# A call order for SyncE, other steps in the up-projection, and which late tap comes first

## The chip, the cores and the metric

The kernel runs on one core of one Trainium2 chip, in one launch. The metric is the device time of one execution in microseconds (us). The engines are named as in the profile: PE is TensorE, DVE is VectorE, ACT is ScalarE, POOL is GpSimd, SP is SyncE, which only issues DMAs.

## The reference

Two layers (`l` = 0, 1) of an encoder over 1024 tokens of width 1024, in float32, and a last norm. Cut to what matters here:

```
for l in range(2):
    h = rmsnorm(x);  p = h @ w_in
    q, k, v from the normed latents of p (384 and 256 wide), 8 heads of 64 + 32 rotary
    y_attn = softmax(q k^T) v
    u = a * sigmoid(g)                     # 512 channels
    u = depthwise_conv(u, 31 taps)
    u = silu(layernorm(u))
    x = x + concat(y_attn, u) @ w_o
    z = depthwise_conv(rmsnorm(x) @ w_up, 3 taps)     # 1024 x 5632
    zg, zv = split(z)
    x = x + (silu(zg) * zv) @ w_down       # 2816 x 1024
return rmsnorm(x)
```

## The kernel before

Activations lie with channels on the 128 partitions and the 1024 tokens along the free dimension. To keep float32's accuracy, an operand is split into an upper part ("hi", rounded to the type TensorE multiplies) and a lower part ("lo", the rest), and a product is three matmuls: hi·hi, hi·lo, lo·hi. Each layer runs through projection, attention, output projection (wo), up-projection and down-projection. In layer 0 these begin at about 0, 200, 421, 507 and 920 us, layer 1's attention at about 1320 and its up-projection at 1628 us.

**Who orders the work.** The kernel writes out its order by hand: closures are put on numbered steps with a rank inside the step, and emitted step by step. Inside `tc.manual_schedule(engines=MANUAL)` the engines in `MANUAL` issue their instructions in the order of emission. SP is not among them, so the framework's scheduler orders SP's DMAs by its own estimates of when each can start.

**The up-projection** (`up_steps`). There are 22 blocks `f` of 128 gate features (e = 0) and 128 value features (e = 1). The tokens are in two halves, the 1024 inputs of a weight block too, and a Strassen-like scheme makes the four half-products out of seven (the sets i = 1 to 7) per block. A product (i, f) is 12 matmuls in f16 of 128 x 512 (L1221) and takes one step. The steps are numbered on from the 16 of the wo stage, so the 154 products are steps 16 to 169. The sequence is `START` for the first four blocks (`LEFT`), then for each block the sets in `ORDER`. `at[i, f]` is the step of a product, m = at[1, f] that of a block's first one.

Per block, with distances from m that stand in `UP`:

- `fetch` (SP, L1106): two raw weight blocks of 512 KB, into a buffer "wr" (e = 0) and a buffer "b" (e = 1)
- `squares` (ACT, L1128), one for each e in two steps: squares of the raw weights, for the scale of each feature; `total` (PE, L1161) sums them over the partitions, a step later DVE makes the scale (L1133 and following)
- `first_hi`, `first_lo`: sets 1 and 2, upper on ACT (L1182), lower on DVE (L1185)
- `sum5`, `sum6`, `sum3`, `sum7` (POOL, L1112): DMAs that add another quarter of the weights onto the raw buffer, in place; sum5 comes one step after the first square, sum6 after lo of 5, sum3 after lo of 6, sum7 one step after `first_lo`, onto the e = 0 buffer
- `part_hi`, `part_lo` of the sets 5, 6, 3, 7, 4 (L1182, L1185), the pair of numbers in `UP`. lo of set 7 is the last to read the e = 0 buffer, lo of set 4 the last to read the e = 1 buffer.

One step after a product `evict` takes it out of PSUM: as a copy on ACT (L1228) or as an addition on DVE (L1229). When the three parts of zg are there, the filter of 3 taps starts on ACT (L1618) and is done on DVE (L1624), one tap in each of the next two steps; `silu` (L1260, ACT) and `close` (the product of zg and zv, L1102 by `sub`) follow, and `close` also issues the store of the result to HBM (L1268). For the first four blocks the steps of the filters stand in `TAPS_AT`, gate and value. `sum_load`, `sum_step` (DVE, L1102) prepare sums of the down weights, and the last sum's step also issues their store (L1281).

**The head of attention.** Per head, q's part `pn` is multiplied on TensorE (L234), scaled out of PSUM on DVE (`qn`, L748), split by ACT (`qns`, L750) and DVE (L752); `pv` (L1653) makes v; then the scores `s` (L1677). Beside it, on an agenda `n` spread over attention, the taps of the 31-tap convolution that are left are done as "late" taps (`tap_late`), each with a buffer of its own that must have come free, of three kinds:

- "act": ACT multiplies in two halves (L1906), POOL issues a DMA that adds (L1914)
- "pool": POOL multiplies (L1909) and issues the DMA that adds
- "both": POOL multiplies and adds (L1909, L1912)

`LATE_KINDS` gives the repeating five kinds for the first and for the second half of the taps (50 in layer 0, 48 in layer 1).

Of the kernel before, what the change touches and what calls it, by code (L numbers as in the profile page):

```python
# [31 lines left out]
NF = DFF // 128  # L32
# [44 lines left out]
ROW_AT = {2: (7,)}  # L77
ROW_LATE = {0: (6,)}
E = mybir.EngineType
MANUAL = [E.PE, E.DVE, E.Activation, E.Pool]  # L80
LATE_KINDS = (("pool", "both", "act", "pool", "act"), ("pool", "both", "pool", "pool", "pool"))
LATE_COST = {"act": 1.1, "pool": 3.5, "both": 4.8}
NEAR_TAPS = (12, 14, 16, 14)
NEAR_ORDER = (0, 1, 2, 3)
# [2 lines left out]
NPAR = P_BF + 2 * NF  # L87
HALVES = (slice(0, 512), slice(512, T))
ORDER = (1, 5, 6, 3, 7, 2, 4)
LEFT = 4  # L90
START = [(i, f) for f in range(LEFT) for i in (1, 2)]
START += [(i, f) for i in (5, 3, 6, 7, 4) for f in range(LEFT)]
MIX_AT = {5: (((19, 1), (20, 0.5)), ((20, 0.4), (21, 0.5))), 3: (((23, 0.6), (24, 0.6)), ((24, 0.5), (25, 0.6))),
          6: (((26, 0.6), (27, 0.6)), ((27, 0.5), (28, 0.6))), 7: (((30, 0.6), (31, 0.6)), ((31, 0.5), (32, 0.6))),
# [3 lines left out]
KEPT = 18  # L98
TAIL_STEPS = 6
FIRST_TOTAL = 7  # L100
TOTAL_AT = 32
TAPS_AT = (36, 39, 42, 46), (44, 48, 52, 57)
UP = {'fetch': -18, 'squares': -15, 'total': -13, 1: (-2, -2), 5: (-10, -9), 6: (-5, -4), 3: (0, 1), 7: (2, 3), 4: (-1, 0)}
SUM_AT = (0, 1, 2, 6)
LEFT_AT = {5: (15, 16, 18, 19), 6: (19, 21, 22, 23), 3: (24, 25, 26, 27), 7: (25, 31, 33, 34), 4: (37, 38, 39, 40)}
ENDS = (slice(512, 768), slice(768, T))
LEAD_HEADS = 3
# [26 lines left out]
class Encoder:  # L134
# [257 lines left out]
    def run(self):  # L392
# [11 lines left out]
        carry = None  # L404
        with self.tc.manual_schedule(engines=set(MANUAL)):
            for l in range(DEPTH):
# [687 lines left out]
    def up_steps(self, l, steps, put):  # L1094
        nc, a = self.nc, self.a
        left, right = HALVES
        seq = START + [(i, f) for f in range(LEFT, NF) for i in ORDER if (i, f) not in START]
        base = len(steps)
        at = {p: base + q for q, p in enumerate(seq)}
        self.kept = {}  # L1100
        raw, wts, zs, st, sums, scale, back, nback = defaultdict(dict), {}, defaultdict(dict), {}, {}, {}, {}, {}
# [28 lines left out]
        def scales(ps, out, w):  # L1130
            ps = ps.rearrange("p (f e) -> p f e", e=2)
            scale, back, nback, v, h = (out[:, i * w:(i + 1) * w] for i in range(5))
            nc.vector.tensor_reduce(out=v, in_=ps, op=ALU.add, axis=AX.X)  # L1133
            self.half_exponent(h, v)
            self.power(scale, h, -1.0, 204.0)
            for o, at in ((back, self.back), (nback, self.nback)):
                nc.vector.tensor_scalar(out=o.bitcast(I32), in0=h.bitcast(I32), scalar1=EXPONENT, scalar2=at, op0=ALU.mult, op1=ALU.add)
            return scale, back, nback

        def first_total():  # L1140
            ps = self.bank(f"wt{l}", (128, 2 * LEFT))
            tags = self.banks[1][0]
            tags.insert(0, tags.pop())
            nc.tensor.matmul(ps, self.ones, st["sums"], start=True, stop=True)
            parts = scales(ps, self.cp.tile([128, 5 * LEFT], F32, name=f"wt{l}", tag="wt", bufs=1), LEFT)
            for f in range(LEFT):
                scale[f], back[f], nback[f] = (t[:, f:f + 1] for t in parts)
# [97 lines left out]
        def filter_start(f, e):  # L1245
            z = zs[f]
            z["ov"[e]] = o = self.blk(f"{'ov'[e]}{l}_{f}")
            z["in", e] = z.pop("gv"[e]) if e == 0 else z["src"]
            self.conv_start(l, e * NF + f, o, z["in", e], 0, T)

        def filter_tap(f, e, t):
            z = zs[f]
            self.conv_tap(l, e * NF + f, z["ov"[e]], z["in", e], 0, T, t)

        def keep(f):
            zs[f]["src"] = zs[f].pop("v")

        def silu(f):
            o = zs[f]["o"]
            nc.scalar.activation(out=o, in_=o, func=AF.Silu)  # L1260

        def close(f):
            z = zs.pop(f)
            sub(z["v"], z["v"], z["o"], ALU.mult)
            if f >= KEPT:
                self.kept[f] = z["v"]
                return
            nc.sync.dma_start(out=self.actd[l][f], in_=z["v"])  # L1268

        def sum_load(j):  # L1270
            sums[j] = [self.blk(f"sd{l}_{j}{e}") for e in range(2)]
            for e, t in enumerate(sums[j]):
                nc.sync.dma_start(out=t, in_=a["w_down"][l, j + e * (NF // 2)])

        def sum_step(j, n):
            p, q = sums[j]
            o, x = ((p[:, left], p[:, right]), (p[:, right], q[:, right]), (q[:, right], p[:, left]), (q[:, left], q[:, right]))[n]
            sub(o, o, x, ALU.add)
            if n == 3:
                for e, t in enumerate(sums.pop(j)):  # L1280
                    nc.sync.dma_start(out=self.wsd[l][j, e], in_=t)  # L1281

        def at_step(m, rank, g, *args):
            put(m, rank, lambda: g(*args))
# [11 lines left out]
        for f in range(LEFT):  # L1296
            at_step((13, 13, 15, 15)[f], 6 + f, sum5, f)
            for i, ms in LEFT_AT.items():
                m, g = ms[f], f % 2
# [4 lines left out]
        for q, (i, f) in enumerate(seq):  # L1304
            n = base + q
            steps.append(lambda i=i, f=f: product(i, f))
            m = EVICT.get((i, f), n + 1)
            put(int(m), m % 1 * 10, lambda i=i, f=f: evict(i, f))
        for f in range(LEFT, NF):
            n = m = at[1, f]  # L1310
            for e in range(2):
                at_step(m + UP["fetch"], 5 + e / 10, fetch, f, e, "b" if e else "wr")
                at_step(m + UP["squares"] + e, 2, own_squares, f, e)
            at_step(m + UP["squares"] + 1, 2.1, sum5, f)
            at_step(max(m + UP["total"], TOTAL_AT), 0.4, own_total, f)
            at_step(max(m + UP["total"], TOTAL_AT) + 1, 0.5, own_scale, f)
            for i in (5, 6, 3, 7, 4):
                hi, lo = (max(m + o, TOTAL_AT + 1) for o in UP[i])
                at_step(hi, 3.6, part_hi, i, f)
# [7 lines left out]
        for f in range(NF):  # L1327
            n = max(at[2, f], at[3, f], at[6, f]) + 1
            n = n if f >= LEFT else TAPS_AT[0][f]
            put(n, 3, lambda f=f: filter_start(f, 0))  # L1330
            put(n + 1, 3, lambda f=f: filter_tap(f, 0, 0))
            put(n + 2, 3, lambda f=f: filter_tap(f, 0, 2))
            put(n + 3, 4, lambda f=f: silu(f))
            m = max(at[7, f], at[4, f]) + 2 if f >= LEFT else TAPS_AT[1][f]
            put(m, 2.9, lambda f=f: keep(f))
            put(m, 3, lambda f=f: filter_start(f, 1))
            put(m + 1, 3, lambda f=f: filter_tap(f, 1, 0))
            put(m + 2, 3, lambda f=f: filter_tap(f, 1, 2))
            put(max(m + 3, n + 5), 3, lambda f=f: close(f))
        for j in range(NF // 2):  # L1340
            n = at[1, 7 + j * 13 // 11]
            put(n - 4, 5, lambda j=j: sum_load(j))
            for i, d in enumerate(SUM_AT):
                put(n + d, 4, lambda j=j, i=i: sum_step(j, i))

    def down_steps(self, l, steps, put):
        nc, a = self.nc, self.a
# [63 lines left out]
        def product(i, j, ms=range(4), cs=done):  # L1411
            b, t = pairs[i, j], BANK_SET[i]
            for m in ms:
                if i in (1, 5, 2) and j == 0:
                    ps[t, m] = self.pp.tile([128, 512], F32, name=f"pd{l}_{i}{m}", tag=f"d{4 * t + (m + 2) % 4}", bufs=1)
                for s, (p, q) in enumerate(((0, 0), (0, 1), (1, 0))):
                    nc.tensor.matmul(ps[t, m][:, cs], w[i, j][p][:, m * 128:(m + 1) * 128], b[:, q, cs],  # L1417
                                     start=(i in (1, 5, 2) and j == 0 and s == 0), stop=(j == half - 1 and s == 2),
                                     skip_group_check=i in (6, 7, 4, 3))
# [19 lines left out]

        order = [(i, j) for i in ORDER for j in range(half)]  # L1440
        at = {p: base + q for q, p in enumerate(order)}
# [27 lines left out]
        for c in range(2 if last else 0):  # L1469
            for m in range(4):  # L1470
                steps.append(lambda c=c, m=m: [product(4, j, (m,), cols[c]) for j in range(tail, half)])
        for i in ORDER[:-1]:
            for m in range(4):
# [166 lines left out]
    def attention(self, l, u, conv, away, spill, kvs, loaded, ahead, wo, begun):  # L1640
# [162 lines left out]
        while any(rest.values()):  # L1803
            j = max((j for j in rest if rest[j]), key=lambda j: (all(j != e for e, _ in late[-2:]), len(rest[j]), -j))
            late.append((j, rest[j].pop(0)))
        kinds = [LATE_KINDS[2 * i // len(late)][i % 5] for i in range(len(late))]
        costs, taken = [LATE_COST[kind] for kind in kinds], set()
# [247 lines left out]
```

## Time and profile before

| | us |
|---|---|
| median of 3 runs | 2264.53 |
| lowest, highest | 2263.61, 2265.57 |
| the profiled execution | 2264.85 |
| its span in the profile | 2263.0 |
| TensorE busy | 2233.7 |
| mean granted clock of TensorE | 0.999 |

The page gives each engine's busy time and the costliest groups of instructions. A group's row has: line, engine, operation, out<-in by the program's names without numbers, shapes and count; then busy us and mean ns; then the idle time of the engine just before these instructions, and who ended most of it. A row of a timeline has the start, the length, then the same, and in brackets the idle time before it and its releaser. A row of waits has who waited for whom: us in total, how often, the longest. "SPq" and "POOLq" are the queues of DMA issues.

### The profile page before, as it was taken

The page shows a single profiled execution, that of the slowest core. Times are in us where ns is not written, and L with a number is a line of the kernel's source. Part 1 is how long each engine was busy: PE and PEld are TensorE (multiplying, and loading weights), DVE is VectorE, ACT ScalarE, POOL GpSimd, SP SyncE. Part 2 cuts the span into 40 slices and gives each one's busy share as a digit, 9 for nine tenths or more (in the row PEclk, how much of TensorE's full clock was granted, in tenths as well). Part 3 has the DMA queues.
Part 4 walks back from the last instruction along what each step waited for, and adds up shares of the span by engine and source line. Part 5 has one row for each costly group of instructions (what it writes and reads, how often), then busy time and mean ns, then how long its engine had stood idle before and what let it go on. Part 6 is the DMA issues. An engine that isn't in the chain of part 4 may idle for free.

```text
span 2263.0 us, 30127 instructions
## 1 busy us (share of the span) xinstructions
PE 2233.7 (99%) x10762; PEld 1511.4 (67%) x10762; DVE 1809.0 (80%) x2484; ACT 1349.5 (60%) x2076; POOL 659.2 (29%) x632
## 2 busy tenths in 40 slices
PE   9999999999999999999999999999999999999998
PEld 8887777784444444788888877777744444448887
DVE  7989888878888887776559798887798887878665
ACT  5355987646766665544533568786467666655444
POOL 1222788511111111001412237864111111110032
PEclk9999999999999999999999999999999999999999
DMA  6887998955589796835968989878646888868356
GB/s 192 171 182 251 196 205 176 267 152 117 134 231 257 202 255 163 295 102 138 210 142 167 212 252 208 182 158 246 168 108 158 236 244 223 241 162 284 103 123 171
DMA packets 176967, 434.81 MB, mean 192 GB/s; under 512 B 24769, under 2 KB 32817, under 8 KB 176817
## 3 DMA queue, kind: packets, MB, share of 16 engines
q0 software_dynamic: 79520, 176.31, 41.7%
q1 hardware_dynamic: 97008, 256.04, 33.5%
q8 instruction: 85, 1.39, 0.3%
q14 instruction: 66, 0.53, 0.1%
q10 hardware_dynamic: 288, 0.53, 0.1%
HBM read 293.56 MB, written 80.40 MB: 165 GB/s over the span
## 4 chain that ended last, share of the span: by engine, by line
PE 71%; DVE 12%; DMA 8%; ACT 4%; issue 4%; POOL 1%; SPq 0%; DVEq 0%; POOLq 0%; ACTq 0%
PE pd L1417 18%; PE p L1221 18%; PE s L1677 7%; DMA wu<-in_w_up 5%; PE po L956 5%; PE t L1717 4%; PE o L1740 4%; PE pa L234 2%; DVE w L1185 2%; DVE v L1624 2%; PE pg L234 2%; PE pg L552 2%; DVE conv L1892 2%; PE pq L234 1%; DVE sd L1102 1%
## 5 line engine op out<-in xcount | busy, mean ns | idle before, releaser
L1221 PE MATMUL p<-b,w 128*128 128x512 f16 x3696 | 807.6, 379 | 16.6 <-DVE w L1185 12.1
L1221 PEld LDWEIGHTS <-w 128*128 128x128 f16 x3696 | 360.3, 99 | 449.0 <-DVE w L1185 22.5
L1417 PE MATMUL pd<-ab,wd 128*128 128x512 f32 (+1 forms) x1920 | 422.7, 382 | 0.0
L1417 PEld LDWEIGHTS pd<-ab,wd 128*128 128x128 f32 x1920 | 350.7, 188 | 69.7 <-DVE ab L1612 0.4
L1112 POOL DMA_DIRECT2D wu<-in_w_up x176 | 153.7, 945 | 757.2 <-DVE w L1185 370.4
L1677 PE MATMUL s<-k,q 96*128 96x512 f32 x768 | 208.2, 406 | 3.3 <-DVE qn L748 3.0
L1128 ACT ACTIVATE wsq<-wu 128x1024 f16<-128x1024 f32 x88 | 92.3, 1050 | 179.8 <-DMA wu<-in_w_up 159.3
L1720 DVE SCALAR_TENSOR_TENSOR pt<-t,pt 128x512 f16<-128x512 f32 x256 | 164.7, 684 | 39.2 <-ACT pt L1719 38.6
L1185 DVE SCALAR_TENSOR_TENSOR w<-wu,wf,w 128x512 f16<-128x512 f32 (+1 forms) x216 | 177.4, 834 | 14.6 <-ACT w L1182 14.6
L1909 POOL TENSOR_TENSOR late<-gate,par 128x1014 f32<-128x1014 f32 (+12 forms) x79 | 172.4, 2182 | 12.8 <-PE pn L234 7.1
L1719 ACT ACTIVATE pt<-t 128x512 f16<-128x512 f32 x256 | 139.2, 595 | 56.8 <-PE t L1717 55.9
L1182 ACT ACTIVATE w<-wu,wf 128x512 f16<-128x512 f32 (+1 forms) x216 | 162.5, 783 | 6.9 <-DMA wu<-in_w_up 6.8
L1679 DVE TENSOR_REDUCE mx<-s 128x1 f32<-128x1024 f32 x128 | 155.6, 1215 | 1.3 <-PE s L1677 1.3
L1624 DVE SCALAR_TENSOR_TENSOR o<-zg,par,o 128x1023 f32<-128x1023 f32 x88 | 112.6, 1280 | 53.9 <-ACT o L1618 53.7
L1677 PEld LDWEIGHTS s<-k,q 96*128 96x128 f32 x768 | 135.8, 189 | 26.4 <-DVE qn L748 3.4
L1892 DVE SCALAR_TENSOR_TENSOR conv<-gate,par,conv 128x1009 f32<-128x1009 f32 (+7 forms) x112 | 142.2, 1274 | 3.7 <-ACT conv L614 1.0
L1687 ACT ACTIVATE p<-s,mx 128x1024 f32<-128x1024 f32 x128 | 143.3, 1119 | 2.6 <-DVE mx L1679 2.2
L1610 ACT CAST ab<-ac 128x512 fp32r<-128x512 f32 x130 | 80.0, 616 | 101.6 <-DVE ac L1351 64.3
L1717 PEld LDWEIGHTS t<-ident,p 128*128 128x128 f32 x1024 | 119.7, 141 | 25.1 <-DVE yt L1747 0.8
L1740 PE MATMUL o<-pt,v 128*128 128x512 f16 x512 | 132.8, 381 | 1.3 <-DVE pt L1720 1.1
L1717 PE MATMUL t<-ident,p 128*128 128x128 f32 x1024 | 133.2, 273 | 0.1
L918 POOL DMA_DIRECT2D wd<-in_w_down x44 | 31.8, 724 | 323.6 <-PE pd L1417 322.4
(2114 smaller groups left out, 3834.9 us busy)
## 6 DMA issues: line engine op xcount, KB each, us to landing
wu<-in_w_up SPq DMA_DIRECT2D x98, 512.0 KB, 5.9
wu<-in_w_up POOLq DMA_DIRECT2D x176, 256.0 KB, 4.7
sd<-in_w_down SPq DMA_DIRECT2D x44, 512.0 KB, 6.6
ws<-sd SPq DMA_DIRECT2D x44, 512.0 KB, 4.2
wd<-in_w_down POOLq DMA_DIRECT2D x88, 256.0 KB, 5.5
act<-v SPq DMA_DIRECT2D x36, 512.0 KB, 4.5
ac<-act SPq DMA_DIRECT2D x72, 256.0 KB, 5.8
wo<-in_w_o POOLq DMA_DIRECT2D x64, 256.0 KB, 7.5
```

The source lines that it names most:

```text
L1182: nc.scalar.activation(out=t, in_=src, func=AF.Copy, scale=scale[f])
L1185: nc.vector.scalar_tensor_tensor(out=t, in0=src, scalar=scale[f], in1=hi, op0=ALU.mult, op1=ALU.subtract)
L1221: nc.tensor.matmul(ps, w[p][:, k * 128:(k + 1) * 128], b[:, q], start=(i in (1, 5, 2) and k == 0 and t == 0), stop=(k == 3 and t == 2), sk ...
L1417: nc.tensor.matmul(ps[t, m][:, cs], w[i, j][p][:, m * 128:(m + 1) * 128], b[:, q, cs], start=(i in (1, 5, 2) and j == 0 and s == 0), stop= ...
L1624: self.nc.vector.scalar_tensor_tensor(out=o[:, a:b], in0=z[:, at + a:at + b], scalar=self.par[l][:, tap:tap + 1], in1=o[:, a:b], op0=ALU.m ...
L1677: nc.tensor.matmul(ps[:, cs], q[i][0:96, qs], k[j][0:96, cs], start=(s == 0), stop=(s == 2))
L1679: nc.vector.tensor_reduce(out=mx, in_=ps, op=ALU.max, axis=AX.X, negate=True)
L1717: nc.tensor.transpose(tp[:, i, qi * 128:(qi + 1) * 128], st["p"][2 * qp + qi][:, kt * 128:(kt + 1) * 128], self.ident)
L1720: nc.vector.scalar_tensor_tensor(out=lo, in0=tp, scalar=P_SCALE, in1=hi, op0=ALU.mult, op1=ALU.subtract)
L1740: nc.tensor.matmul(po, v[2 * c + i][:, h // 2, e, :], pt[s][:, 2 * (c % 2) + i, :], start=(c == 0 and i == 0 and s == 0), stop=(c == 3 and ...
L1892: self.nc.vector.scalar_tensor_tensor(out=y[:, lo:hi], in0=u[:, lo + s:hi + s], scalar=self.tap(l, j, t), in1=y[:, lo:hi], op0=ALU.mult, o ...
L1909: self.nc.gpsimd.tensor_tensor(out=p[:, lo:hi], in0=u[:, lo + s:hi + s], in1=self.tap(l, j, t).broadcast_to([128, hi - lo]), op=ALU.mult)
```

## The change

1. SP joins `MANUAL`: its DMAs are issued in the order of emission. The two stores become closures of their own (`act_store`, `sum_store`), one step (`STORE_LAG`) after `close` and after the last `sum_step`.
2. In the first half of the late taps the kinds go act, both, pool, act, pool and not pool, both, act, pool, act; their numbers in five stay.
3. From the fifth block on the up-projection takes the sets in `UP_ORDER`: set 2 is second, 6 third, 5 fourth; 7 stays fifth, 3 goes from fourth to sixth, 4 stays last. `START` exchanges (2, 0) and (1, 1). The down-projection keeps `ORDER`.
4. In `UP`, squares, total, and the parts of 5, 6, 3 and 4 come one step later, lo of 7 and hi of 7 one step earlier; `TOTAL_AT` and `TAPS_AT` for the first four blocks change.

```diff
-MANUAL = [E.PE, E.DVE, E.Activation, E.Pool]
-LATE_KINDS = (("pool", "both", "act", "pool", "act"), ("pool", "both", "pool", "pool", "pool"))
+MANUAL = [E.PE, E.DVE, E.Activation, E.Pool, E.SP]
+LATE_KINDS = (("act", "both", "pool", "act", "pool"), ("pool", "both", "pool", "pool", "pool"))
...
 ORDER = (1, 5, 6, 3, 7, 2, 4)
+UP_ORDER = (1, 2, 6, 5, 7, 3, 4)
 LEFT = 4
-START = [(i, f) for f in range(LEFT) for i in (1, 2)]
+START = [(i, f) for i, f in ((1, 0), (1, 1), (2, 0), (2, 1), (1, 2), (2, 2), (1, 3), (2, 3))]
...
-TOTAL_AT = 32
-TAPS_AT = (36, 39, 42, 46), (44, 48, 52, 57)
-UP = {'fetch': -18, 'squares': -15, 'total': -13, 1: (-2, -2), 5: (-10, -9), 6: (-5, -4), 3: (0, 1), 7: (2, 3), 4: (-1, 0)}
+TOTAL_AT = 33
+TAPS_AT = (35, 37, 40, 46), (41, 47, 54, 60)
+UP = {'fetch': -18, 'squares': -14, 'total': -12, 1: (-2, -2), 5: (-9, -8), 6: (-4, -3), 3: (1, 2), 7: (1, 2), 4: (0, 1)}
 SUM_AT = (0, 1, 2, 6)
+STORE_LAG = 1
...
-        seq = START + [(i, f) for f in range(LEFT, NF) for i in ORDER if (i, f) not in START]
+        seq = START + [(i, f) for f in range(LEFT, NF) for i in UP_ORDER if (i, f) not in START]
...
-            nc.sync.dma_start(out=self.actd[l][f], in_=z["v"])
+            st["act", f] = z["v"]
+
+        def act_store(f):
+            if f < KEPT:
+                nc.sync.dma_start(out=self.actd[l][f], in_=st.pop(("act", f)))
...
-            if n == 3:
-                for e, t in enumerate(sums.pop(j)):
-                    nc.sync.dma_start(out=self.wsd[l][j, e], in_=t)
+
+        def sum_store(j):
+            for e, t in enumerate(sums.pop(j)):
+                nc.sync.dma_start(out=self.wsd[l][j, e], in_=t)
...
             put(max(m + 3, n + 5), 3, lambda f=f: close(f))
+            put(max(m + 3, n + 5) + STORE_LAG, 3, lambda f=f: act_store(f))
...
+            put(n + SUM_AT[-1] + STORE_LAG, 4, lambda j=j: sum_store(j))
```

## The prediction

> **What bounds the kernel now.** I read the page first, then the busy time of the two up-projections, then who makes TensorE wait, then the timelines around the largest of these waits, and last the waits of SyncE's queue.
>
> ```profile
> span 2263.0 us, 30127 instructions
> ...
> PE 2233.7 (99%) x10762; PEld 1511.4 (67%) x10762; DVE 1809.0 (80%) x2484; ACT 1349.5 (60%) x2076; POOL 659.2 (29%) x632
> ...
> L1221 PE MATMUL p<-b,w 128*128 128x512 f16 x3696 | 807.6, 379 | 16.6 <-DVE w L1185 12.1
> ...
> L1128 ACT ACTIVATE wsq<-wu 128x1024 f16<-128x1024 f32 x88 | 92.3, 1050 | 179.8 <-DMA wu<-in_w_up 159.3
> ...
> wu<-in_w_up SPq DMA_DIRECT2D x98, 512.0 KB, 5.9
> wu<-in_w_up POOLq DMA_DIRECT2D x176, 256.0 KB, 4.7
> ```
>
> TensorE is busy for 2233.7 of 2263.0 us. The change gives it no other matmuls, so all that can be won is its idle time, 29.3 us, what each stop costs beside it, and time at a low granted clock. More than half of the idle time stands before the products of the up-projection (L1221). The two stages, layer 0 and layer 1:
>
> ```profile
> 507.10:920.30 413.20, 404.69 (x1898) 185.76 (x1898) 342.30 (x478) 262.73 (x370) 70.43 (x80) 1.00 0.74 196
> 1627.70:2040.70 413.00, 404.86 (x1898) 185.80 (x1898) 342.44 (x479) 262.37 (x370) 69.31 (x80) 1.00 0.75 196
> ```
>
> The columns after the length are the busy times of PE, PEld, DVE, ACT and POOL. PE is idle for 8.51 and 8.14 us, 16.65 together; DVE is 83% busy and ACT 64%, so neither is the bound on average and the idle time is one of order. TensorE's waits name the places:
>
> ```profile
> PE p L1221 <- DVE w L1185: 12.1, 15, 1.6
> PE p L1221 <- ACT zg L1228: 3.0, 3, 1.3
> PE s L1677 <- DVE qn L748: 3.0, 1, 3.0
> PE p L1221 <- DVE b L1034: 1.3, 2, 0.6
> ```
>
> Twenty stops (15, 3 and 2) lie in the up-projections; in total 16.4 us, none longer than 1.6. One more, of 3.0 us, is at the start of layer 0's attention. A stop costs more than its idle time, since a lone matmul shows 379 ns, but in a run they follow each other faster:
>
> ```profile
> 749.67 8.15 PE L1221 MATMUL p<-b,w 128*128 128x512 f16 x37
> ...
> 764.28 0.59 PE L1221 MATMUL p<-b,w 128*128 128x512 f16 x2 [1.15 <-ACT zg L1228]
> ```
>
> (8.15 − 0.38) / 36 = 0.216 us, so each stop adds 0.38 − 0.22 = 0.16, twenty of them 3.3. Removable in both up stages: 16.65 + 3.3 = 19.9 us. A step is 12 matmuls, 12 × 0.216 = 2.59 us: longer than any stop.
>
> **Up-projection: the late weights.** The stop above is the end of this chain (ACT, then POOL, then DVE):
>
> ```profile
> 749.60 1.06 ACT L1128 ACTIVATE wsq<-wu 128x1024 f16<-128x1024 f32 x1 [5.05 <-DMA wu<-in_w_up]
> ...
> 761.38 1.33 ACT L1182 ACTIVATE w<-wu,wf 128x512 f16<-128x512 f32 x2 [2.83 <-DMA wu<-in_w_up]
> ...
> 763.57 0.67 ACT L1228 ACTIVATE zg<-p,wf 128x512 f32<-128x512 f32 x1
> ```
> ```profile
> 754.70 0.87 POOL L1112 DMA_DIRECT2D wu<-in_w_up  x1 [2.29 <-ACT wsq L1128]
> ```
> ```profile
> 762.75 0.75 DVE L1185 SCALAR_TENSOR_TENSOR w<-wu,wf,w 128x512 f16<-128x512 f32 x1 [2.80 <-ACT w L1182]
> ```
>
> ScalarE stands 5.05 us at its square, because the block it squares was fetched only three steps earlier; behind that wait in its queue lie the evictions of PSUM. sum5, issued after the squares, lands late, ScalarE waits 2.83 us more, and the eviction at 763.57 releases the product at 764.28. The page puts 159.3 us of such waits before the squares in all. After the change the squares come four steps after the fetch, so one step, 2.59 us, is taken off each such wait, and sum5, hi and lo of sets 5 and 6 move one step later with them, keeping their own distances. Set 6 stays third and 5 goes from second to fourth, so both lower halves still stand five steps or more ahead of their products. Also the slot of the fetch comes free sooner, as lo of set 7 (its last reader on that side) moves from +3 to +2:
>
> ```profile
> SPq L1106 <- DVE w L1185: 193.2, 38, 30.0
> SPq L1281 <- DVE sd L1102: 148.9, 29, 10.3
> SPq L1268 <- DVE v L1102: 116.9, 36, 19.1
> ```
>
> The first row says that fetches do wait for that reader (38 times), so its moving gives the fetch about another step. The price is on the other side: sum7 is now two steps ahead of hi7 and not three. By the page's 4.7 us to landing after an issue of 0.87 that is 5.6 against 2 × 2.59 = 5.2 us from step to step; hi7 stands behind an eviction (0.67), a square (1.06), a filter start and hi3 in its own step, over 3 us of ScalarE's work, so I cost it at nothing. Without that cover ScalarE would wait about 0.4 us per block, and lo7 has the slack for that, as follows.
>
> **Up-projection: set 7 and DVE.** Fifteen of the twenty stops wait for L1185, the lower half of set 7 in nearly all. It is issued one step before its product now; the product keeps its place (+4), lo7 moves from +3 to +2. The largest stop:
>
> ```profile
> 592.64 1.28 DVE L1624 SCALAR_TENSOR_TENSOR o<-zg,par,o 128x1023 f32<-128x1023 f32 x1
> 593.83 0.75 DVE L1185 SCALAR_TENSOR_TENSOR w<-wu,wf,w 128x512 f16<-128x512 f32 x1
> ```
> ```profile
> 594.64 8.59 PE L1221 MATMUL p<-b,w 128*128 128x512 f16 x39 [1.60 <-DVE w L1185]
> ```
>
> DVE is behind with filter taps of the first four blocks. Here the new TAPS_AT counts as well: a tap is due one and two steps after each start, so in the four steps up to lo7 of block 4 there were taps at 44, 45, 46 and 47; now it is only the one at 43 in the four steps up to 46. Three taps, 3.8 us, go from ahead of it, against a stop of 1.60. For block 5 likewise (50, 53 and 54 up to its lo7 at 54 before; none from 50 to 53 after). lo3 and lo7 and an eviction of set 2 now fall in one step: 2 × 0.75 + 0.75 + about 1.3 for a tap, some 3.6 us after that step's start, against 5.2 to the product: 1.6 us left, which also takes the 0.4 of hi7. Set 2 second in the START list takes the two stops on L1034 (0.65 each), since (2, 0) comes a step later than the end of its operand.
>
> Sum for the up stages: between 0 and 19.9. I take 16: the distances grow by a whole step where no stop is above 1.6, and I leave 2 us per layer for collisions that I can't place (new spots where DVE has 4.2 us of work in a step).
>
> **Attention's first late tap.** Around layer 0's start, PE, DVE, POOL, and the stretch after:
>
> ```profile
> 194.76 0.62 PE L234 MATMUL pn<-cqs_2h,wu10l 128*128 128x512 f32 x2
> 195.22 0.62 PE L234 MATMUL pn<-cqs_2l,wu10h 128*128 128x512 f32 x2
> ...
> 199.52 0.39 PE L1653 MATMUL pv<-wv0h,kvs_1l 128*128 128x512 f32 x1
> 202.91 1.66 PE L1677 MATMUL s<-k,q 96*128 96x512 f32 x6 [3.00 <-DVE qn L748]
> ```
> ```profile
> 195.69 6.03 DVE L752 SCALAR_TENSOR_TENSOR qn<-qn,qns 128x1024 fp32r<-128x1024 f32 x2
> 201.65 1.21 DVE L748 TENSOR_TENSOR qn<-pn,rq 128x1024 f32<-128x1024 f32 x1
> ...
> 1318.28 2.43 DVE L752 SCALAR_TENSOR_TENSOR qn<-qn,qns 128x1024 fp32r<-128x1024 f32 x2
> ```
> ```profile
> 195.47 2.06 POOL L1909 TENSOR_TENSOR late<-gate,par 128x1023 f32<-128x1023 f32 x1 [5.71 <-DMA q<-rc]
> ...
> 198.44 2.19 POOL L1909 TENSOR_TENSOR late<-gate,par 128x1020 f32<-128x1020 f32 x1
> 200.71 3.24 POOL L1912 TENSOR_TENSOR conv<-conv,late 128x1020 f32<-128x1020 f32 x1
> ```
> ```profile
> 203.00:210.00 7.00, 7.00 (x24) 5.57 (x25) 5.97 (x11) 6.08 (x11) 0.95 (x1) 0.76 1.02 379
> ```
>
> Two L752 take 6.03 us here and 2.43 in layer 1, where no POOL operation runs beside them. The first began 0.2 us after POOL's multiply, the second during the next one; each ended about 1.1 us, its own length, after the POOL operation did. So L748 is late by 3.6, TensorE stops for 3.00, and then 7.00 us of matmuls run at a granted clock of 0.76, which is 7.00 × 0.24 = 1.7 us lost. The Trainium skill, "SBUF — State Buffer", section "SBUF: two separate sides", states the same as a rule: DVE with two SBUF inputs and GpSimd share a port pair, and whoever starts first holds it for its whole instruction. By that rule the change doesn't remove the conflict, it leaves one of the two blockings, and the trace agrees with the whole-instruction hold (2.9 against 1.2 us for each L752).
>
> With ScalarE's tap first, POOL's first operation is the multiply of the tap after it, whose buffer comes free with the last of these matmuls on pn, at 195.84 and not at 195.38 (cqs_2l and cqs_2h hold the first two buffers of the late taps). It would start at about 195.9, after L752 has begun at 195.69. Then three outcomes: both L752 go ahead of POOL (end 198.1, L748 at 199.3, no stop); POOL goes between them (to 199.1, L752 to 200.3, L748 to 201.5, a stop of 1.7); or nothing changes (3.0). I take a stop of 1.0, between the first two, and full clock after it, because the stops of 1.60 in the up stage leave its clock at 1.00 in the window rows: 2.0 + 1.7 = 3.7, from 0 to 4.7. ScalarE's two halves of the tap move some steps earlier, at the same count in each five taps; it has idle time there (6.08 of 7.00 busy), so nothing. Layer 1's stop is not seen in the waits; nothing.
>
> **SyncE in order.** Nothing in a trace of before shows this order. Removing the freedom costs between nothing and the slack of the fetch. Stores are issued a step later, so that the queue's head doesn't stand at L1268 and L1281 for DVE's last sum (116.9 and 148.9 us of waits now, up to 19.1). What stands behind a waiting head is the next fetch, with four steps (10.4 us) to its square and 5.9 to land: 4.5 us of slack. I take zero, with a chance for the rest below.
>
> **Sum.** The profiled execution took 2264.85 (span 2263.0 and 1.85 around it), the median of the runs 2264.53: no correction. 2264.85 − 16 − 3.7 = 2245.
>
> **Rivals.**
> *The queue's head (slower).* A fetch waits up to 30.0 us for its slot; in order, all SyncE's transfers stand behind it. If the next fetch is so held more than the 4.5 us beyond its planned step, the squares wait, ScalarE's evictions behind them are late, and each further us goes into TensorE, for 18 blocks in two layers. At 1 us over: +36 − 20 = +16, 2281; even at 0.55 us. For: 193.2 us of waits on slots. Against: the slot frees earlier now, and the loads of later blocks need the same slots in the same order anyway. The Trainium skill, "DMA: Bandwidth & Descriptors", section "Anatomy of one DMA — SWDGE (gpsimd) path", says that the wait for a semaphore is made by the issuing sequencer, not the DMA engine; that is what would make this happen, and L1106's row shows such waits. 0.17.
> *DVE keeps the stops.* Its work is the same 342 us per stage, now with two lower halves in one step; the stops move from set 7 to the evictions of set 2 and the gain is the attention's alone: 2261 (−0.17%). For: 83% busy. Against: it has 71 us idle per stage. 0.09.
> *Nothing at attention, up stage as forecast:* 2249. Inside the range.
>
> **Numbers.** Forecast 2245, 0.74 with its neighbours from 2240 (all 19.9 + 4.7 = 24.6 won) to 2255. The range 2240 to 2266 takes in the second rival and leaves out most of the first. A change of 0.2% (4.5 us) is about what a measurement of this kernel can tell. Faster 0.74, same 0.09, slower 0.17.
>
> **What would show it.** Right: PE's waits on L1185 in the up stages fall from 12.1 to under 3 us, those on zg and on L1034 go; ScalarE's wait before the squares falls well under 159.3; the two L752 at 195.7 take under 4.5 us, PE's stop at s is under 2 and the stretch after it is at clock 1.00. Wrong: SyncE's waits at L1106 grow and ScalarE's wait before the squares with them; or PE's stops in the up stage name an eviction or a sum of set 3 or 7.

## The result, and the profile after

The changed kernel takes 2241.95 us (median of 4 runs, 2241.17 to 2243.32), the kernel before 2264.54; the ratio is 0.9901 with a 95% interval of 0.9884 to 0.9918. Its profiled execution took 2243.32 us, the longest of the four. The changed kernel's code stands 2 lines further down ahead of the new closures (L1185 is L1187, L748 is L750) and 9 behind them (L1677 is L1686).

The page, and the busy time in the two up-projections from first to last product (length, then PE, PEld, DVE, ACT, POOL):

```profile
span 2241.4 us, 30140 instructions
...
L1223 PE MATMUL p<-b,w 128*128 128x512 f16 x3696 | 803.6, 379 | 0.0
```
```profile
506.20:908.90 402.70, 402.70 (x1898) 186.43 (x1898) 342.42 (x478) 267.02 (x370) 69.94 (x80) 1.00 0.74 197
1615.96:2018.70 402.74, 402.74 (x1898) 186.46 (x1898) 342.39 (x478) 267.12 (x370) 68.86 (x80) 1.00 0.73 197
```

TensorE has no idle time left in front of any of the 3696 matmuls. The stages are 10.5 and 10.3 us shorter, with the same work on DVE (342 us). ScalarE's wait before the squares, 159.3 us in the kernel before, has come down to this:

```profile
ACT wsq L1130 <- DMA wu<-in_w_up: 8.7, 4, 2.9
```

What TensorE still waits for, the whole view:

```profile
PE lnp L1945 <- DVE yt L1756: 2.2, 2, 1.9
PE o L1749 <- DVE pt L1729: 1.1, 2, 0.6
PE warm L425 <- DVE ones_r L401: 1.1, 1, 1.1
PE s L1686 <- DVE qn L750: 1.0, 1, 1.0
PE po L958 <- DVE wt L1135: 0.5, 2, 0.3
PE rx_768p L263 <- DVE xss L1360: 0.2, 1, 0.2
PE t L1726 <- ACT p L1696: 0.2, 1, 0.2
```

The stop before s has gone from 3.0 to 1.0 us. The first row is new: lnp, at the end of attention. The head of layer 0's attention, on DVE, POOL and PE, and then the same ten microseconds of before and after (PE busy first, the granted clock is the third number from the end):

```profile
195.72 4.05 DVE L754 SCALAR_TENSOR_TENSOR qn<-qn,qns 128x1024 fp32r<-128x1024 f32 x2
199.69 1.21 DVE L750 TENSOR_TENSOR qn<-pn,rq 128x1024 f32<-128x1024 f32 x1
```
```profile
196.00 2.69 POOL L1918 TENSOR_TENSOR late<-gate,par 128x1020 f32<-128x1020 f32 x1 [6.21 <-PE pn L236]
```
```profile
200.96 1.67 PE L1686 MATMUL s<-k,q 96*128 96x512 f32 x6 [0.97 <-DVE qn L750]
```
```profile
200.00:210.00 10.00, 7.09 (x24) 5.66 (x25) 8.83 (x13) 6.14 (x11) 3.87 (x2) 0.83 1.04 366
```
```profile
200.00:210.00 10.00, 9.04 (x38) 7.16 (x39) 8.74 (x16) 8.43 (x17) 2.00 (x1) 1.00 1.03 420
```

Two DVE operations take 4.05 and not 6.03 us. POOL's multiply starts at 196.00, behind the first of them, and ends at 198.69; the second ends 1.1 us later. One of the two blockings is left, and the clock is not lowered any more.

The balance by profiles: 10.5 + 10.3 in the up-projections and 2.0 + 1.7 at attention's head are 24.5, less 2.2 at lnp is 22.3; the spans differ by 21.6. The 0.7 between them isn't placed.

### The profile page after: what moved, and what is told of

Same layout as the page of the kernel before. It is cut to its first block, busy times and chain, and to the rows that moved or that the text cites. A ratio compares the mean times of both kernels' runs of the same rounds, so it can differ in the third digit from the quotient of the medians.

```text
span 2241.4 us, 30140 instructions
## 1 busy us (share of the span) xinstructions
PE 2228.5 (99%) x10762; PEld 1511.7 (67%) x10762; DVE 1806.3 (81%) x2484; ACT 1360.0 (61%) x2078; POOL 655.3 (29%) x631
## 4 chain that ended last, share of the span: by engine, by line
PE 94%; DMA 3%; DVE 1%; ACT 1%; issue 0%; SPq 0%; POOL 0%; DVEq 0%; POOLq 0%; ACTq 0%
PE p L1223 36%; PE pd L1426 19%; PE po L958 7%; PE s L1686 7%; PE o L1749 4%; PE t L1726 4%; PE pq L236 3%; PE pa L236 3%; PE pkv L236 2%; PE pg L236 2%; PE pg L554 2%; DMA wo<-in_w_o 1%; PE pk L236 1%; PE pa L554 1%; PE pn L236 1%; PE pv L1662 1%
## 5 line engine op out<-in xcount | busy, mean ns | idle before, releaser
L1686 PE MATMUL s<-k,q 96*128 96x512 f32 x768 | 207.7, 406 | 1.0 <-DVE qn L750 1.0
L1187 DVE SCALAR_TENSOR_TENSOR w<-wu,wf,w 128x512 f16<-128x512 f32 (+1 forms) x216 | 177.0, 833 | 4.0 <-ACT w L1184 4.0
L1918 POOL TENSOR_TENSOR late<-gate,par 128x1016 f32<-128x1016 f32 (+11 forms) x78 | 168.9, 2166 | 13.8 <-PE pn L236 13.8
L1686 PEld LDWEIGHTS s<-k,q 96*128 96x128 f32 x768 | 135.2, 189 | 23.9 <-DVE qn L750 1.4
L1627 ACT ACTIVATE o<-zg,par 128x1024 f32<-128x1024 f32 x44 | 54.5, 1238 | 135.1 <-DVE zg L1231 135.1
```

Source lines behind the costliest of these rows:

```text
L1187: nc.vector.scalar_tensor_tensor(out=t, in0=src, scalar=scale[f], in1=hi, op0=ALU.mult, op1=ALU.subtract)
L1686: nc.tensor.matmul(ps[:, cs], q[i][0:96, qs], k[j][0:96, cs], start=(s == 0), stop=(s == 2))
L1918: self.nc.gpsimd.tensor_tensor(out=p[:, lo:hi], in0=u[:, lo + s:hi + s], in1=self.tap(l, j, t).broadcast_to([128, hi - lo]), op=ALU.mult)
```

## The experiments

Each ran beside the kernel before on its own chip; since that one's median went from 2262.67 to 2265.07, the ratios are compared. The last columns are the two up-projections in the profiled execution, from first to last product.

| kernel | us | ratio, 95% interval | up l = 0 | up l = 1 |
|---|---|---|---|---|
| before | 2264.5 | 1 | 413.2 | 413.0 |
| changed | 2241.95 | 0.9901 [0.9884, 0.9918] | 402.7 | 402.7 |
| sp_only | 2298.79 | 1.0162 [1.0147, 1.0178] | 430.5 | 429.2 |
| late_only | 2260.51 | 0.9988 [0.9979, 0.9997] | 414.4 | 412.4 |
| up_only | 2243.88 | 0.9918 [0.9903, 0.9933] | 402.7 | 402.7 |
| sp_squares | 2261.77 | 0.9985 [0.9976, 0.9995] | 409.7 | 410.4 |
| sp_swap | 2293.75 | 1.0129 [1.0114, 1.0144] | 426.2 | 426.5 |
| undo_squares | 2254.47 | 0.9955 [0.9940, 0.9970] | 409.1 | 408.5 |
| undo_set7 | 2253.80 | 0.9953 [0.9937, 0.9970] | 408.6 | 407.4 |
| undo_order | 2247.06 | 0.9920 [0.9905, 0.9935] | 404.4 | 404.1 |
| undo_taps | 2243.94 | 0.9908 [0.9893, 0.9922] | 403.7 | 403.7 |
| y_later | 2240.90 | 0.9904 [0.9887, 0.9920] | 402.7 | 402.7 |
| after_again | 2241.63 | 0.9894 [0.9877, 0.9910] | 402.7 | 402.7 |
| y_again | 2241.64 | 0.9897 [0.9882, 0.9912] | 402.7 | 402.7 |

**One part alone.**

sp_only: the kernel before with the two stores as closures of their own and

```diff
-MANUAL = [E.PE, E.DVE, E.Activation, E.Pool]
+MANUAL = [E.PE, E.DVE, E.Activation, E.Pool, E.SP]
+STORE_LAG = 1
```

> SyncE in emission order with the stores split off, everything else as before. Parts add up: the up-projections keep their 20 stops (idle about 8.5 and 8.1 us), the first late tap costs 3.0 us again, and a stop of about 2 us appears at lnp, at the end of layer 0's attention, since the loads of y come ahead of the fetches: 2266. Rival, the queue's order is what freed the up-projections: their idle time falls by half or more, 2254 or less. Rival, the queue's head: SyncE's waits hold the fetches and the up-projections stop for longer, 2270 or more.

Measured 2298.79, 36 us more than before: the parts do not add up. 17.3 + 16.2 us of it are in the up-projections, where TensorE now stops in most blocks. Its waits, and then one block on ACT:

```profile
PE p L1223 <- ACT zg L1230: 24.5, 25, 1.8
PE p L1223 <- DVE w L1187: 17.6, 25, 1.6
```
```profile
669.06 1.33 ACT L1184 ACTIVATE w<-wu,wf 128x512 f16<-128x512 f32 x2 [2.22 <-DMA wu<-in_w_up]
...
671.25 0.67 ACT L1230 ACTIVATE zg<-p,wf 128x512 f32<-128x512 f32 x1
...
678.75 1.06 ACT L1130 ACTIVATE wsq<-wu 128x1024 f16<-128x1024 f32 x1 [5.18 <-DMA wu<-in_w_up]
```

It is the chain of before, and it now stops TensorE on zg in 19 of the 36 blocks after the first four of each layer, where it did so in 3: ScalarE waits for the fetch and for sum5, and an eviction of zg stands behind in its queue. The stop of about 2 us that was expected at lnp isn't there: 0.4 us. What SyncE issues for one block, before (first) and in sp_only:

```profile
645.90 1.15 SPq L1273 DMA_DIRECT2D sd<-in_w_down  x2
647.14 4.20 SPq L1106 DMA_DIRECT2D wu<-in_w_up  x2
```
```profile
652.80 0.33 SPq L1108 DMA_DIRECT2D wu<-in_w_up  x1
653.22 0.92 SPq L1279 DMA_DIRECT2D sd<-in_w_down  x2
654.23 0.38 SPq L1108 DMA_DIRECT2D wu<-in_w_up  x1
654.71 0.72 SPq L1274 DMA_DIRECT2D act<-v  x1
655.48 3.96 SPq L1288 DMA_DIRECT2D ws<-sd  x2
```

Before, loads of sd and one fetch went out ahead of the fetch that waits for DVE's lower half; in order, six transfers of 512 KB leave within 7 us behind it. The DMA engines' busy tenths between 640 and 900 us, in 40 slices, turn from even to bursts; before, then sp_only:

```profile
DMA  8979988989988987778659979889879969665408
```
```profile
DMA  9389599689769949939949859939939949957947
```

late_only:

```diff
-LATE_KINDS = (("pool", "both", "act", "pool", "act"), ...
+LATE_KINDS = (("act", "both", "pool", "act", "pool"), ...
```

> Only the order of the late taps' kinds as in the change. Parts add up: the stop before s in layer 0 is about 1 us and the clock after it stays at 1.00, 3.7 us gained: 2260.8. Rival, the shorter stop was won by the other parts (a queue that is earlier): the stop stays at 3.0 us, 2264.5.

Measured: 2.2 us less than before on its chip by the medians, 0.7 to 4.8 by the interval, which takes in the 3.7 expected. The stop is 0.97 us, the clock of the ten microseconds after it 1.00, and the first product of layer 0 starts at 503.8 and not at 507.1. That is the changed kernel's attention with no other part of the change. Its up-projections stop as those of the kernel before do.

up_only: the new `UP_ORDER`, `START`, `UP`, `TOTAL_AT` and `TAPS_AT`; SP not in `MANUAL`, old `LATE_KINDS`.

> Only the up-projection's steps and sets as in the change; SyncE is ordered by the scheduler and the late taps go as before. Parts add up: both up-projections run in about 402.8 us, no stop at lnp: 2264.5 - 20.7 = 2243.8. Rival, the queue's order is needed for it: fetches of the scheduler come late for some blocks, up-projections of 406 us or more, 2250 or more.

Measured 2243.88, 18.8 us less than before on its chip. The up-projections are as short without the queue's order as with it, and there is no stop at lnp. At attention's head stand the 3.0 us again, and the clock:

```profile
200.00:210.00 10.00, 7.03 (x25) 5.60 (x25) 8.82 (x13) 5.81 (x11) 3.95 (x2) 0.83 1.04 365
```

So the profiles agree, and those of the other runs do too: 0.83 in these ten microseconds in the five kernels with a stop of 2.9 to 3.0 us (before, up_only and the three whose names start with sp), 1.00 in the nine with one of 0.9 to 1.0. The Trainium skill, "TensorE: Matmul & The Clock Gate", Part 1, puts the idle window that lowers the clock at about 3.4 us; here a stop of 3.0 was enough. The product of the two ratios, 0.9918 x 0.9988 = 0.9906, is the changed kernel's 0.9901 within its interval: beside the other two parts the order of SyncE's queue is worth nothing that can be measured.

**Why the order costs 36 us alone and nothing there.**

sp_squares is sp_only with the extra step of the squares:

```diff
-TOTAL_AT = 32
+TOTAL_AT = 33
-UP = {... 'squares': -15, 'total': -13, 5: (-10, -9), 6: (-5, -4), ...}
+UP = {... 'squares': -14, 'total': -12, 5: (-9, -8), 6: (-4, -3), ...}
```

> sp_only with squares, total and the parts of sets 5 and 6 one step later, as in the change; sets 3, 7, 4, the sequence and the taps as before. If the extra step is what makes the queue's order harmless: the stops on zg go, those on the lower half of set 7 stay (12 us of idle time and 2.4 of restarts), 2256 to 2264. If lo of set 7, which still frees the fetch's slot at +3, keeps the fetch late: stops on zg stay, 2275 or more.

Measured 2261.77: one step more between fetch and square takes the 36 us back. ScalarE's wait before the squares is 9.9 us, against 193.6 in sp_only. The stops on zg are all but gone, those on set 7 stay:

```profile
PE p L1223 <- DVE w L1187: 8.7, 13, 0.9
...
PE p L1223 <- ACT zg L1230: 0.4, 2, 0.2
```

sp_swap is sp_only with the block's two fetches exchanged:

```diff
-                at_step(m + UP["fetch"], 5 + e / 10, fetch, f, e, "b" if e else "wr")
+                at_step(m + UP["fetch"], 5 - e / 10, fetch, f, e, "b" if e else "wr")
```

> SyncE in order alone, as in sp_only, but of the two fetches of a block the one for the value features (e = 1), whose buffer has long been free, is emitted ahead of the one for the gate features (e = 0), which waits for lo of set 7 three blocks earlier, and of the loads of sd. If sp_only's 36 us came of the second fetch standing behind the waiting first one: the second square and sum5 are early again, 2262 to 2270. If they came of the order of the other transfers, or of the first fetch alone: 2290 or more.

Measured 2293.75, 29 us more than before on its chip: 7 of the 36 us come back. My theory, that the second fetch behind the first one is the cause, explains no more than those. In this kernel the second square no longer waits, but the first still does (5.02 us in this block), and so does hi of set 5, for sum5; the eviction behind it stops TensorE for 1.3 us:

```profile
671.12 1.33 ACT L1184 ACTIVATE w<-wu,wf 128x512 f16<-128x512 f32 x2 [3.00 <-DMA wu<-in_w_up]
...
673.31 0.67 ACT L1230 ACTIVATE zg<-p,wf 128x512 f32<-128x512 f32 x1
```

The sums (POOL's DMAs) land later in all kernels with the order: between 640 and 900 us their median from issue to landing is 5.1 us before, 6.3 in sp_only, 7.6 here. In sp_squares it is 8.3, and it does no harm, and in the changed kernel 7.2. That the bursts are what delays the sums is argued from this, not shown: no run spread the transfers alone. Shown is that the step alone makes the kernel before proof against the order.

**One part undone in the changed kernel.**

undo_squares: `squares`, `total`, 5 and 6 and `TOTAL_AT` back.

> The changed kernel with squares, total and the parts of sets 5 and 6 one step earlier, as before; SyncE in order, lo of set 7 early. SyncE in order alone had made the up-projections 17 us longer each, through squares that wait for their fetch. If the squares' extra step is what makes the order harmless: ScalarE's wait before the squares is back (100 us or more), stops in most blocks, 2255 to 2280. Rival, the fetch's slot that comes free a step sooner through lo of set 7 is enough: under 2244.

Measured 2254.47, 0.54% more than the changed kernel and just under the range. The stops on zg are back, 9.1 us, but only 13 of them in 36 blocks. And ScalarE waits mostly for the sums and not, as expected, for the fetch:

```profile
ACT w L1184 <- DMA wu<-in_w_up: 61.0, 30, 3.9
...
ACT wsq L1130 <- DMA wu<-in_w_up: 23.6, 30, 4.5
```

In sp_only the wait for the fetch was 193.6 us with the squares at the same step. So the other steps of the change already take most of it away. The fetch's slot, which comes free a step sooner here, may be the reason, but other steps and the sequence differ too. It is not enough: the rival's "under 2244" did not come.

undo_set7: `7: (2, 3)` back.

> The changed kernel with hi and lo of set 7 at +2 and +3, as before. If the late lower half was the stop and its step is what removes it: stops on L1187 in most blocks, about 0.5 us each, 2250 to 2262. If it matters through the fetch's slot as well: ScalarE's wait before the squares grows, and stops name zg too, 2262 or more. Rival, the spread of DVE's evictions by the new sequence of sets is enough: under 2245.

Measured 2253.80, 0.52% more. Fifteen stops, all on set 7's lower half:

```profile
PE p L1223 <- DVE w L1187: 5.0, 15, 0.9
```

None is on zg, and the squares wait 11.6 us in all: with the squares a step later it does not matter that the fetch's slot comes free a step later too. The stages are 5.9 and 4.7 us longer. The trace has more stops than the view of waits names, 24 on these products, 6.3 us, most of them of 0.15 to 0.19; with the prediction's 0.16 for each restart, 3.8, that makes 10.1 of the 10.6. So a stop that short costs about twice its idle time. The largest stops of before, at (7, 4) and (7, 5), are not among them.

undo_order: `UP_ORDER = ORDER`.

> The changed kernel with the sets in the sequence 1, 5, 6, 3, 7, 2, 4 from the fifth block on; all weights at the steps of the change, so lo of set 3 (+2) stands one step before its product (+3). If the sequence matters only by what DVE has to do in which step: DVE's three additions fall in the steps +4, +5 and +6 again, small stops at set 3, 2244 to 2252. If the steps of the weights do all of it: 2242.

Measured 2247.06 (2244.10 to 2249.16). The up-projections are 1.7 and 1.3 us longer, by five small stops that name evictions of zv, not set 3's lower half; the profiled execution, 2249.16, has also 3.5 us of stops at lnp. In the stages the sequence is worth 3 us.

undo_taps: the old `TAPS_AT`.

> The changed kernel with the taps of the first four blocks at their old steps. If the stops at the products (7, 4) and (7, 5), 1.6 and 1.4 us in each layer, came of DVE's backlog of these taps: lo of set 7, one step sooner, waits behind them still in part; stops up to 1.5 us at two places of each layer, 2243 to 2248. If the step of lo7 alone removes them: 2242, no stop.

Measured 2243.94. One stop of 0.8 us per layer, at the product (4, 5), on an eviction by DVE. The stops at (7, 4) and (7, 5), 1.6 and 1.4 us before, stay away with the old taps too, as they do in undo_set7 with the new taps and set 7 at its old steps: with the rest of the change in place, either is enough.

**The new stop at lnp.** Where it comes from, in the changed kernel (ACT, then PE):

```profile
418.36 0.63 ACT L199 ACTIVATE wo<-wo 128x512 fp32r<-128x512 f32 x1 [2.69 <-DMA wo<-in_w_o]
419.01 0.68 ACT L1755 ACTIVATE yt<-o,sc 64x512 f32<-64x512 f32 x1
```
```profile
420.54 0.51 PE L1945 MATMUL lnp<-lns0h,ones_r 128*128 128x512 f32 x1 [1.86 <-DVE yt L1756]
```

A part of w_o lands late, and yt stands behind its conversion. SyncE issues 12 loads of y behind the fetches of w_up in the kernel before (first) and ahead of them in the changed kernel:

```profile
408.45 6.75 SPq L1106 DMA_DIRECT2D wu<-in_w_up  x3
415.41 7.73 SPq L948 DMA_DIRECT2D y<-in_x  x12
```
```profile
393.32 12.63 SPq L950 DMA_DIRECT2D y<-in_x  x16
407.36 4.78 SPq L1108 DMA_DIRECT2D wu<-in_w_up  x3
```

The order alone doesn't make the stop: sp_only issues the loads of y early too and has 0.4 us at lnp. late_only has none either. y_later and y_again put the loads behind again:

```diff
-        put(-3, 0, load_x)
+        put(0, 9, load_x)
```

> The changed kernel, with the loads of the last 12 pieces of y per layer issued behind the first fetches of w_up and not ahead of them. If the stop of 1.9 us at lnp comes from wo's last loads sharing the DMA engines with these loads: the stop goes, 2240. If wo's loads are only issued too late for an attention that ends earlier: the stop stays, 2242. If y is then late itself: PE stops in the output projection, 2244 or more.

> The changed kernel again, beside the next one on the same chip: 2242, with a stop of 1 to 2 us at lnp.

> The changed kernel with the loads of y behind the first fetches, as in y_later: no stop at lnp, 1 to 2.5 us less than the changed kernel in this call. If the stop at lnp is only filled by another wait: the same time.

The stop at lnp is in the changed kernel's both profiles (2.2 and 1.5 us) and in neither of the other two. But no time is won that can be measured: on one chip 2241.64 against 2241.63. In y_again's profile, its slowest execution (2244.18), another stop stands in layer 1:

```profile
PE po L958 <- DVE us_0l L1979: 1.8, 1, 1.8
```

ScalarE's wait for w_o between 395 and 450 us is 3.4 us in the changed kernel, 4.6 in y_later and 4.4 before; it stands in front of yt or further down its queue. y_later's profile has no such stop (0.5 us at the same place), and its span is 2.1 us shorter than the changed kernel's. So that another wait always fills the place is not shown; shown is that the medians don't move.

## Why the prediction was right, and where it wasn't

Forecast 2245, measured 2241.95. In the profiles the up-projections gave 4.8 us more than forecast, and the stop at lnp and the 0.7 that isn't placed took 2.9 of that back.

- **Up-projection, forecast 16, measured 20.8.** The 19.9 stand for a floor of (826.2 − 19.9) / 2 = 403.1 us per stage, which was right to 0.4. What was mis-sized are the 4 us left for collisions that couldn't be placed: there were none. Set 7's step keeps away the stops on (7, f) from block 6 on and the squares' step those on zg, each shown by undoing it; that (2, 0) behind (1, 1) takes those on L1034 is seen only in the profile, which has them no more.
- **The taps.** Three taps out of DVE's way were counted as a cause of the gain at blocks 4 and 5. undo_taps shows that they were not needed there once set 7's lower half came earlier, and undo_set7 that they, or another part, would have done without it. What they add to the changed kernel is about 1 us per layer, at another product. (In the count for block 5 the tap at 50 lies outside the four steps up to 54.)
- **sum7 closer to hi7, at nothing.** Right: ScalarE's waits for sums in the up stage are 0.2 us between 640 and 900. It is the cover by ScalarE's queue that held, not the time to land: a sum7 issued at 650.64 lands at 658.48, 7.8 us later and not 4.7, and hi7 starts at 659.48, behind an eviction, a square, a filter start and hi3. In three blocks between 640 and 700 us 1.0, 1.0 and 0.0 us are left there, so it is close.
- **The late tap, 2.0 + 1.7.** The stop of 1.0 came out at 0.97. Of the three outcomes it was the second, POOL between the two DVE operations, but POOL's multiply ended at 198.69 and not at 199.1, so that the stop was shorter than the 1.7 worked out for it. That the clock stays up behind it was right. One reading was wrong: in layer 1 a POOL multiply does run beside the two L752. It starts at 1319.75, after the second of them (1319.48), and it is POOL's that is stretched there, to 2.71 us.
- **SyncE's order, at nothing.** The sum came out right, the reason given did not carry it. The 4.5 us of slack were reckoned with the squares' new distance, and it was not said what the order costs without it. sp_only shows it: 36 us, by a mechanism near that of the rival "the queue's head". That its price is the same, 36 us at 1 us for each of 36 blocks, is luck: stops on zg lie in 19 blocks, and others follow them. The argument used against this rival was that the slot of the fetch comes free earlier; undo_set7, where it doesn't, has no stop on zg, and undo_squares, where it does, has 13. The argument that holds is the squares' step.
- **What was not forecast:** the stop at lnp. The loads of y are SyncE's DMAs too and are moved past the fetches and beside POOL's loads of w_o; they were not followed to their place. The loads' place is one condition, as y_later shows by moving it back. An attention that ends earlier is probably the other: only kernels with both the order and the new late taps have 1 us or more of this stop.

## What to carry to other kernels

A change of several parts is not the sum of them: here one part costs 36 us alone and nothing beside another that gives the same wait one step more. Where stops are each shorter than a step, and the engines behind them have idle time, one step of distance at the right operations removed them all here; look in the trace for the operation that stands just in time, and move that. Before a queue is put in a fixed order, follow each of its transfers to its new place, and count the slack of the load that will stand behind a waiting one.

## What the runs showed of the hardware

A DVE operation with two SBUF inputs (L752, 1.22 us alone) that meets a POOL operation already running ends 1.1 us after it does, about its own length, in each of the three meetings at layer 0's head (two before, one after). At layer 1's head two more do the same: 3.63 us from 1323.01 before, 2.99 from 1311.62 after. In the first of these two POOL's record starts 0.35 us after DVE's, so the recorded starts don't always tell who will wait. The sums of 256 KB by POOL's queue took from 5.1 us (median, the kernel before) to 8.3 (sp_squares) to land, while the core moved 196 and 194 GB/s in layer 0's stage: about the same bytes in the same time. The other transfers are bunched differently; that this is the reason is not shown. A stop of 2.9 to 3.0 us was followed by a granted clock of 0.83 over ten microseconds in all five kernels that had it; one of 0.9 to 1.0 at the same place left it at 1.00 in nine, and one of 1.60 in the up-projection of the kernel before left it at 1.00 between 592 and 597.
